# An attention kernel on one core: the probabilities' product with the mask is read from SBUF and stands behind the split of the next weights, and two late tiles' values are moved on

## The chip, the cores and the metric

The kernel runs on one core of one Trainium2 chip. The metric is device time in microseconds (us) of one execution of the whole program. A core has five engines with a queue each, which are worked in order: TensorE (PE in the profile; its weight loads are PEld), VectorE (DVE), ScalarE (ACT), GpSimd (POOL) and SyncE (SP). SP and POOL issue the DMA transfers here. The memory on the core is SBUF; TensorE's results land in PSUM.

## The reference

One step of a small decoder for a prompt of 1024 positions and 8 single-token samples, model width 2048, all in float32. With the sizes of this case it has one pooling layer and one attention layer. The attention layer is the one that the change touches:

```python
z = x @ w_in                                   # queries (32 heads x 64) and gate
q = rope_partial(z[..., :D_ATTN], pos)         # rotation of 16 of 64 dimensions
s = einsum('qkgd,skd->kgqs', q, k) * 64 ** -0.5
s = where((kp <= qp) & (qp - kp < 128), s, -1e30)        # window of 128
m = maximum(max(s), sink)
p = exp(s - m);  p = p / (sum(p) + exp(sink - m))
o = einsum('kgqs,skd->qkgd', p, v)
y = (o * silu(gate)) @ w_out
x = layer_norm(ALPHA * x + y)
```

Keys and values are shared by groups of 8 heads and are projected once.

## The kernel before, in words

**Tiling.** Activations lie transposed: channels on the 128 partitions, positions along the free dimension, in two chunks c = 0 (512 columns) and c = 1 (512 columns and the 8 samples). The program runs through ten phases. Each phase multiplies a stream of weight blocks (128 x 1024) with one chunk. A float32 product is made of three faster ones: every weight block is cast by ScalarE to a high part (line 488, `cast_to`), VectorE takes the rest (line 503, the "split", in `prep_to`), and TensorE multiplies high by high, high by low and low by high (lines 658 to 660, or 686 to 688).

**Runs and units.** Most phases use Strassen's scheme with seven products: one `run` is one weight block, 24 matmuls. Two phases are "plain": there a `unit` makes one output tile from two blocks of 24 matmuls. The attention projections are three phases: chunk 0, heads tiles t = 0 to 7 (plain), chunk 0, t = 8 to 15 (seven products), and chunk 1, t = 0 to 15 (seven products). A tile t is two heads.

**What sets the order.** The program is written out in full by Python, and each engine's order is the order in which the functions record. A step counter `self.i` goes on by one at `end()`: after each run, and twice within each block of a unit (so a unit is four steps). `begin()` starts a block: it flushes `posts` (evictions of the last results and the like), loads blocks ahead on SP's queue, casts and splits the next block (`prep_to`), and casts further ahead. `end()` puts in TensorE's side work that is due at this step (`product`, by rank) and then the other engines' (`at`).

**Attention beside the projections.** `attend(c, t, at, s1, s2, late)` puts a tile's attention between the projections' runs, at steps counted from its call: `score` (line 1760, TensorE, into the PSUM tile `S`) at step `at`; `select` and `largest` (lines 1778 to 1790), `expo`, `total`, `norm` (lines 1797 to 1810) in the next steps; `turn` (line 1814, eight transposes into `PT`, the first half of `S`) at `at + s1`; `keep`; and `values0` (line 1848) at `at + s1 + s2`. `keep` makes two SBUF tiles from `PT`: ScalarE's copy `w` (line 1823) and VectorE's product with a constant mask, `wp` (line 1824). With s2 = 2 `keep` is recorded at the end of the step after the transposes, with s2 = 1 it is put into `posts`. `values` has two parts; each needs `w` for its first four matmuls and `wp` from the fifth on. Part 1 comes after part 0, and in many steps the next tile's score stands between them. `late` says where the values land in PSUM: in the second half of `S`, or in tiles of their own. `gate` (line 1876) then multiplies with the gate.

**Rotation.** A query pair's halves are exchanged by DMA (line 1616, on SP's queue); VectorE then makes the rotation, two products (line 1624) and a sum (line 1731), and a small copy for the samples (line 1735). `q_done` records it three steps after the projection, at the end of a step. The next score needs it.

**Sums of weight blocks.** The seven products need sums of blocks. They are made by VectorE the first time (line 293 in the plain phase, line 346 in the next one, with a store on POOL's queue) and read back later; for the output projection they are made on the side (lines 436 to 441).

Of the kernel before, what the change touches and what calls it, by code (L numbers as in the profile page):

```python
# [16 lines left out]
P = 128  # L17
# [77 lines left out]
class Slot:  # L95


    def __init__(self, mem, i, h, a):
        self.mem, self.i, self.h, self.a = mem, i, h, a
# [82 lines left out]
class Kern:  # L182
    def __init__(self, ctx, tc, io):
        self.tc, self.io = tc, io
        self.nc = tc.nc
        pool = lambda name, **kw: ctx.enter_context(tc.tile_pool(name=name, **kw))
        one = pool("one", bufs=1)
        self.smp = pool("smp", bufs=2)
        dram = pool("dram", bufs=1, space=bass.MemoryType.DRAM)
        self.psd = [pool(f"psd{i}", bufs=1, space=bass.MemoryType.PSUM) for i in range(3)]  # L190
        self.pso = pool("pso", bufs=1, space=bass.MemoryType.PSUM)
        self.four = None
        ctx.callback(self.use_four, None)
        self.prm = one.tile([P, N_PRM], F32, name="prm")
        self.cst = one.tile([P, N_CST], F32, name="cst")
        self.mki = one.tile([P, P], I32, name="mki")
        self.jr = one.tile([P, P], F32R, name="jr")
        self.nsink = one.tile([P, NH], F32, name="nsink")
        self.carry = one.tile([P, NK, NST], F32, name="carry")
        self.kdec = one.tile([P, 2, NDEC], F32, name="kdec")  # L200
        self.qd = [one.tile([P, NDEC, 8], F32, name=f"qd{i}") for i in range(2)]
        self.sgd = [one.tile([P, 8, NDEC], F32, name=f"sgd{i}") for i in range(2)]
        self.flag = one.tile([P, 1], F32, name="flag")
        self.mem = Mem(pool("mem", bufs=1), NSLOT)
        self.n = 0
        self.i = self.e = self.lastO = self.turns = self.ring = 0
        self.posts, self.events, self.side = [], {}, []
        self.extra, self.on = None, False
        self.fresh = False
        self.ahead = 7, 4, 3  # L210
        dr = lambda n, s: dram.tile(s, F32, tag=n, name=n)
        self.Td, self.act, self.l_sq, self.l_sh = {}, {}, {}, {}
        for c, (_, T) in enumerate(CHUNKS):
            for n, k in (("x", "ai"), ("g", "ao"), ("h", "bi"), ("o", "bo")):
                if (k, c) in STRASSEN:
                    self.Td[n, c] = dr(f"t{n}{c}", [P, 8, 4, T // 2])
            self.act["x", c] = io[f"x{c}"]
            for n in ("g", "h", "o", "p"):
                self.act[n, c] = dr(f"{n}{c}", [P, NK, T])
        self.gbd = dram.tile([32, 2 * P], F32, tag="gbd", name="gbd")  # L220
        self.ws = {
            n: [dr(f"s{n}{q}", [P, 4, 1024]) for q in range(np_)]
            for n, np_ in (("wia", 16), ("woa", 8), ("wkv", 2), ("wib", 16), ("wob", 8))
        }
# [285 lines left out]
    def flush(self):  # L510
        todo, self.posts = self.posts, []
        for go in todo:
            go()

    def begin(self):
        self.flush()
        a, b, d = self.ahead if self.strassen else (5, 4, 3)
        if getattr(self, "ph", "") == "bi1" and len(self.mem.whole()) < 4:
            a, b, d = min(a, 6), min(b, 3), min(d, 2)
        self.load_to(self.e + a)  # L520
        self.prep_to(self.e + d)
        self.cast_to(self.e + b)
        self.make_to(self.e + b + (1 if self.strassen else 0))
        self.e += 1
        return self.hl.pop(self.e - 1)
# [146 lines left out]
    def unit(self, done):  # L672

        nc = self.nc
        ps = self.psD()
        for par in range(2):
            w = self.begin()
            wh, wl = (s.r for s in w)
            for k in range(8):
                if k == 4:  # L680
                    self.flush()
                s = slice(k * P, (k + 1) * P)
                if k % 2 == 0:
                    x = self.x_get((par, k // 2))
                h, l = (a.rv(2, TP)[:, k % 2, :] for a in x)
                nc.tensor.matmul(ps[:], wh[:, s], h, start=par == 0 and k == 0, stop=False)  # L686
                nc.tensor.matmul(ps[:], wh[:, s], l, start=False, stop=False)  # L687
                nc.tensor.matmul(ps[:], wl[:, s], h, start=False, stop=par == 1 and k == 7)  # L688
                if k % 2:
                    self.x_used((par, k // 2))  # L690
                if k == 7:
                    for a in w:
                        a.free()
                    if par == 1:
                        self.posts.append(lambda: done(ps))
                if k in (3, 7):
                    self.end()
# [1047 lines left out]
    def attend(self, c, t, at, s1, s2, late=False):  # L1745
# [5 lines left out]
        PT = self.S[:, 0, :]  # L1751
        x = {}
# [66 lines left out]
        def keep():  # L1819


            x["w"], x["wp"] = self.mem.full(), self.mem.full()
            nc.scalar.copy(x["w"].a[:, :1024], PT)
            nc.vector.tensor_mul(
                x["wp"].a[:, :1024].rearrange("p (i k) -> p i k", k=P),
                PT.rearrange("p (i k) -> p i k", k=P),
                cst[:, None, K_MP : K_MP + P].to_broadcast([P, 8, P]),
            )

# [30 lines left out]
                x["wp"].free()  # L1860

        def values0():
            values(0)
            if self.i in self.scores:
                self.product(0, 3, lambda: values(1))
                self.at(1, gate)
            else:
                self.product(1, 0, lambda: values(1))
                self.at(1, lambda: self.posts.append(gate))
# [27 lines left out]
        if s2 > 1:  # L1897
            self.at(at + s1 + 1, keep)
        else:
            self.at(at + s1, lambda: self.posts.append(keep))  # L1900
        self.product(at + s1 + s2, 1, values0)

    def gate_done(self, c, t0, s, n):
# [125 lines left out]
    def phase_bi(self, c, ps, nxt):  # L2029
# [4 lines left out]
        if not self.strassen:  # L2034
            for done in (self.k_done, self.v_done):
                box = {}
                for j in range(2):

                    def take(ps, j=j, done=done, box=box):
                        if j == 0:  # L2040
                            box["s"] = self.mem.full()
                        nc.scalar.copy(box["s"].a[:, j * T : (j + 1) * T], ps[:])
                        if j == 1:
                            done(c, box["s"])

                    self.unit(take)
            for t in range(2 * ps[0], 2 * ps[-1] + 2):
                def q_done(ps, t=t):
                    s = self.mem.half()
                    nc.scalar.copy(s.a[:, :T], ps[:])  # L2050
                    self.q_done(c, t, s, 1, 4)

                def g_done(ps, t=t):
                    s = self.mem.half()
                    nc.scalar.copy(s.a[:, :T], ps[:])
                    self.gate_done(c, t, s, 1)

                n = t - 2 * ps[-1]
                self.attend(c, t, 9, *{-1: (11, 1), 0: (13, 2), 1: (8, 2)}.get(n, (14, 2)), n == 0)
                self.unit(q_done)  # L2060
                if t == 2 * ps[-1] - 1:
                    self.x_begin(nxt)
                self.last = t == 2 * ps[-1] + 1
                self.unit(g_done)
            self.last = False
            return
# [295 lines left out]
```

## Time and profile before

| what | value |
|---|---|
| median of 3 runs | 2360.27 us (2354.43, 2361.5, 2360.27) |
| the profiled execution's own time | 2356.38 us |
| its span, first to last instruction | 2354.6 us |
| TensorE busy | 2297.3 us, 98% of the span |
| VectorE busy | 1925.9 us, 82% |
| ScalarE busy | 1343.1 us, 57% |
| mean granted TensorE clock | 0.996 |
| attention beside the projections | about 1158 to 2040 us |

In a row of a group, the numbers behind the bar are the busy time, the mean duration of one in ns, and the idle time of the engine just before them, with what ended most of it. In a row of waits, "A <- B: x, n, m" says that A waited x us for B in n waits, the longest m. In a timeline the columns are start in us, duration in us, engine, line, operation, tiles and shapes, count, and in square brackets the idle time before, with what ended it; rows of one kind are merged. A row of windows has the stretch, its length, the busy time and instructions of PE, PEld, DVE, ACT and POOL, the granted clock, the DMA engines' share and GB/s.

### The profile page before, as it was taken

The numbers are of one execution on the slowest core, as the hardware profiler recorded it, in microseconds if no ns is written. First come the engines' busy times: TensorE is split into PE (matmuls) and PEld (weight loads), VectorE is DVE, ScalarE is ACT, GpSimd is POOL, SyncE is SP. The second block draws the span as 40 slices with busy tenths as digits, with TensorE's granted clock in tenths as the row PEclk, the third lists the DMA queues.
The fourth block names the chain that finished last, engine by engine and source line by source line (L and its number), as shares of the span: only waits on it lengthen the run. The fifth ranks groups of instructions, "written<-read, shape, count | busy, mean of one in ns | idle before, by whom it ended". The sixth has DMA issues, their size and how long they took to land. (4 is left out here: it accounts for less than half of the span.)

```text
span 2354.6 us, 49710 instructions
## 1 busy us (share of the span) xinstructions
PE 2297.3 (98%) x19960; PEld 2200.9 (93%) x19960; DVE 1925.9 (82%) x2421; ACT 1343.1 (57%) x2429; POOL 205.5 (9%) x411
## 2 busy tenths in 40 slices
PE   8999999999999999999999899999999999999997
PEld 6899999999999999998788799999999999999997
DVE  8787998776878878978987788887777768888887
ACT  4444446544546547554465566685666678546556
POOL 0111110001000000000111111100000000000000
PEclk9999999999999999999999999999999999999999
DMA  8668789989889989999786766688777768799785
GB/s 293 211 246 303 271 299 346 332 292 319 289 289 339 327 280 333 328 388 327 272 310 220 248 219 239 224 310 270 237 249 245 230 201 305 239 342 372 260 300 199
DMA packets 250919, 665.18 MB, mean 283 GB/s; under 512 B 25632, under 2 KB 106432, under 8 KB 250688
## 3 DMA queue, kind: packets, MB, share of 16 engines
q1 hardware_dynamic: 205216, 496.94, 63.0%
q0 software_dynamic: 45472, 165.07, 18.1%
q8 instruction: 156, 2.56, 0.4%
q14 instruction: 75, 0.61, 0.1%
HBM read 466.81 MB, written 185.59 MB: 277 GB/s over the span
## 5 line engine op out<-in xcount | busy, mean ns | idle before, releaser
L658 PE MATMUL pD<-m,m 128*128 128x260 f32 (+1 forms) x4752 | 1346.0, 283 | 8.1 <-ACT pD L599 4.4
L660 PE MATMUL pD<-m,m 128*128 128x260 f32 (+1 forms) x4752 | 1339.1, 282 | 4.4 <-DVE m L503 4.4
L659 PE MATMUL pD<-m,m 128*128 128x260 f32 (+1 forms) x4752 | 1338.8, 282 | 0.0
L658 PEld LDWEIGHTS pD<-m,m 128*128 128x128 f32 x4752 | 894.5, 188 | 13.7 <-ACT pD L599 5.5
L660 PEld LDWEIGHTS pD<-m,m 128*128 128x128 f32 x4752 | 895.2, 188 | 5.5 <-DVE m L503 5.5
L503 DVE TENSOR_TENSOR m<-m,m 128x1024 fp32r<-128x1024 f32 x674 | 814.5, 1219 | 100.1 <-ACT m L488 60.6
L659 PEld LDWEIGHTS pD<-m,m 128*128 128x128 f32 x4752 | 894.9, 188 | 0.5
L488 ACT CAST m<-m 128x1024 fp32r<-128x1024 f32 x674 | 702.7, 1049 | 324.7 <-DVE m L346 85.1
L686 PE MATMUL pD<-m,m 128*128 128x512 f32 x448 | 179.7, 401 | 8.0 <-ACT m L769 8.0
L687 PE MATMUL pD<-m,m 128*128 128x512 f32 x448 | 177.9, 397 | 1.0 <-DVE m L778 1.0
L688 PE MATMUL pD<-m,m 128*128 128x512 f32 x448 | 177.5, 396 | 0.0
L778 DVE TENSOR_TENSOR m<-m,m 128x1024 fp32r<-128x1024 f32 (+1 forms) x120 | 147.0, 1226 | 6.4 <-ACT m L769 4.7
L769 ACT CAST m<-m 128x1024 fp32r<-128x1024 f32 (+1 forms) x120 | 125.9, 1053 | 17.7 <-PE pD L687 5.2
L631 ACT COPY m<-pD 128x260 f32<-128x260 f32 (+1 forms) x83 | 31.1, 375 | 179.2 <-PE pD L660 179.1
L346 DVE TENSOR_TENSOR m<-m,m 128x1024 f32<-128x1024 f32 x88 | 107.6, 1222 | 12.7 <-DMA m<-in_wib 6.3
L686 PEld LDWEIGHTS pD<-m,m 128*128 128x128 f32 x448 | 85.1, 190 | 28.1 <-ACT m L769 8.0
L687 PEld LDWEIGHTS pD<-m,m 128*128 128x128 f32 x448 | 85.0, 190 | 21.1 <-DVE m L778 2.1
L688 PEld LDWEIGHTS pD<-m,m 128*128 128x128 f32 x448 | 85.0, 190 | 19.7
L1797 ACT ACTIVATE m<-m,sm 128x128 f32<-128x128 f32 x256 | 99.4, 393 | 0.0
L619 DVE TENSOR_TENSOR m<-pD,m 128x260 f32<-128x260 f32 (+1 forms) x86 | 36.5, 424 | 74.4 <-PE pD L660 74.1
L1088 PE MATMUL pD<-m,m 128*128 128x260 f32 (+1 forms) x528 | 91.5, 323 | 0.0
L1088 PEld LDWEIGHTS pD<-m,m 128*128 128x128 f32 x528 | 79.5, 188 | 8.2
(249 smaller groups left out, 2180.9 us busy)
## 6 DMA issues: line engine op xcount, KB each, us to landing
m<-in_wia SPq DMA_DIRECT2D x124, 512.0 KB
m<-in_wib SPq DMA_DIRECT2D x120, 512.0 KB
swia<-m POOLq DMA_DIRECT2D x64, 512.0 KB, 4.8
m<-swia SPq DMA_DIRECT2D x64, 512.0 KB
m<-swoa SPq DMA_DIRECT2D x64, 512.0 KB
swib<-m POOLq DMA_DIRECT2D x64, 512.0 KB, 5.1
m<-swib SPq DMA_DIRECT2D x64, 512.0 KB
m<-swob SPq DMA_DIRECT2D x56, 512.0 KB
```

The costliest lines, as they stand in the source:

```text
L346: self.nc.vector.tensor_add(s[out].a[:, :1024], s[x].a[:, :1024], s[y].a[:, :1024])
L488: self.nc.scalar.copy(hi.r[:, :1024], self.stream[self.cast].src().a[:, :1024])
L503: self.nc.vector.tensor_sub(lo.r[:, :1024], s.src().a[:, :1024], hi.a[:, :1024])
L658: nc.tensor.matmul(ps[:, :TH], wh[:, s], h, start=new and k == 0, stop=False, skip_group_check=on)
L659: nc.tensor.matmul(ps[:, :TH], wh[:, s], l, start=False, stop=False, skip_group_check=on)
L660: nc.tensor.matmul(ps[:, :TH], wl[:, s], h, start=False, stop=k == 7, skip_group_check=on)
L686: nc.tensor.matmul(ps[:], wh[:, s], h, start=par == 0 and k == 0, stop=False)
L687: nc.tensor.matmul(ps[:], wh[:, s], l, start=False, stop=False)
L688: nc.tensor.matmul(ps[:], wl[:, s], h, start=False, stop=par == 1 and k == 7)
L769: self.nc.scalar.copy(h.r[:, :n], s.a[:, :n])
L778: self.nc.vector.tensor_sub(l.r[:, :n], s.a[:, :n], h.a[:, :n])
L1088: nc.tensor.matmul(ps[:, : cs.stop - cs.start], ws[:, s], d[:, cs], start=f0 and k == 0, stop=l0 and k == 3,)
```

## The change

The mask product reads ScalarE's SBUF copy `w` instead of `PT`. It is no longer recorded in `keep`: `keep` puts it on a list, `behind_prep`, which a new function `settle` empties. `settle` is called in `begin()` behind `prep_to`, in `unit` behind the flush in the middle of a block, and ahead of the values. For the plain phase's tiles 5 (n = -1) and 6 (n = 0) the steps are changed: tile 5's transposes come two steps later, and its values land in the second half of `S`; tile 6's values follow one step behind the transposes instead of two.

```diff
@@ class Kern
+        self.behind_prep = []
...
+    def settle(self):
+        todo, self.behind_prep = self.behind_prep, []
+        for go in todo:
+            go()
+
     def begin(self):
         self.flush()
...
         self.load_to(self.e + a)
         self.prep_to(self.e + d)
+        self.settle()
         self.cast_to(self.e + b)
@@ def unit
                 if k == 4:
                     self.flush()
+                    self.settle()
@@ def keep
             nc.scalar.copy(x["w"].a[:, :1024], PT)
+            self.behind_prep.append(mask)
+
+        def mask():
             nc.vector.tensor_mul(
                 x["wp"].a[:, :1024].rearrange("p (i k) -> p i k", k=P),
-                PT.rearrange("p (i k) -> p i k", k=P),
+                x["w"].a[:, :1024].rearrange("p (i k) -> p i k", k=P),
                 cst[:, None, K_MP : K_MP + P].to_broadcast([P, 8, P]),
             )
@@ def values0
+            self.settle()
             values(0)
@@ def phase_bi
-                self.attend(c, t, 9, *{-1: (11, 1), 0: (13, 2), 1: (8, 2)}.get(n, (14, 2)), n == 0)
+                self.attend(c, t, 9, *{-1: (13, 1), 0: (13, 1), 1: (8, 2)}.get(n, (14, 2)), n in (-1, 0))
```

How this moves instructions is seen in the engines' orders. The changed file is longer, so its line numbers are higher: the mask is line 1824 before and 1835 in the changed kernel, ScalarE's copy 1823 and 1831, the cast 488 and 489, the split 503 and 504, the rotation 1624 and 1632 with its sum 1731 and 1739 and its copy 1735 and 1743, a sum of weight blocks 346 and 347, an eviction 619 and 626. A row is line, operation, result <- operands (the numbers tell buffers apart) and shape.

VectorE in chunk 1, at the transposes of tile 2 (the place is the mask of `keep` and what follows), before:

```order
L503 TENSOR_TENSOR m_2213_20135<-m_2197_19966,m_2210_20090 128x1024
L1824 TENSOR_TENSOR m_2216_20164<-pS_12840,cst 128x1024
L1624 TENSOR_TENSOR m_2188_19835<-m_2188_19835,m_1533_12852 128x1040
L1624 TENSOR_TENSOR m_2203_20041<-m_2203_20041,m_1533_12852 128x1040
L1731 TENSOR_TENSOR m_2188_19835<-m_2188_19835,m_2203_20041 128x1040
L1735 COPY qd_82<-m_2188_19835 128x8x2
L619 TENSOR_TENSOR m_2217_20175<-pD_20046,m_2207_20084 128x260
```

and of the change:

```order
L504 TENSOR_TENSOR m_2213_20133<-m_2197_19964,m_2210_20088 128x1024
L1632 TENSOR_TENSOR m_2188_19832<-m_2188_19832,m_1533_12852 128x1040
L1632 TENSOR_TENSOR m_2203_20039<-m_2203_20039,m_1533_12852 128x1040
L1739 TENSOR_TENSOR m_2188_19832<-m_2188_19832,m_2203_20039 128x1040
L1743 COPY qd_82<-m_2188_19832 128x8x2
L1835 TENSOR_TENSOR m_2216_20162<-m_2215_20161,cst 128x1024
L626 TENSOR_TENSOR m_2217_20172<-pD_20044,m_2207_20082 128x260
```

The mask has moved behind the whole rotation of the next queries, since `keep` and the rotation are recorded at the end of the same step and `settle` only in the next `begin()`.

VectorE in chunk 0, at the transposes of tile 8, before:

```order
L503 TENSOR_TENSOR m_1847_16223<-m_1827_15972,m_1846_16186 128x1024
L1824 TENSOR_TENSOR m_1850_16252<-pS_12840,cst 128x1024
L1624 TENSOR_TENSOR m_1826_15970<-m_1826_15970,m_1533_12852 128x1024
L1624 TENSOR_TENSOR m_1838_16134<-m_1838_16134,m_1533_12852 128x1024
L1731 TENSOR_TENSOR m_1826_15970<-m_1826_15970,m_1838_16134 128x1024
L503 TENSOR_TENSOR m_1853_16266<-m_1835_16098,m_1848_16225 128x1024
```

and of the change:

```order
L504 TENSOR_TENSOR m_1847_16221<-m_1827_15970,m_1846_16184 128x1024
L1632 TENSOR_TENSOR m_1826_15968<-m_1826_15968,m_1533_12852 128x1024
L1632 TENSOR_TENSOR m_1838_16132<-m_1838_16132,m_1533_12852 128x1024
L1739 TENSOR_TENSOR m_1826_15968<-m_1826_15968,m_1838_16132 128x1024
L504 TENSOR_TENSOR m_1853_16263<-m_1835_16096,m_1848_16223 128x1024
L1835 TENSOR_TENSOR m_1850_16250<-m_1849_16249,cst 128x1024
```

Here the mask stands behind the rotation and behind the split of the next block.

ScalarE around the copy of tile 5 in the plain phase, before:

```order
L488 CAST m_1736_15001<-m_1731_14947 128x1024
L1795 ACTIVATE sm_14990<-sm_14990 128x8
L1797 ACTIVATE m_1734_14967,sm_14991<-m_1734_14967,sm_14989 128x128 x4
L769 CAST m_1739_15037<-m_1697_14586 128x1024
L1823 COPY m_1742_15043<-pS_12840 128x1024
L1797 ACTIVATE m_1734_14967,sm_14991<-m_1734_14967,sm_14989 128x128 x4
L769 CAST m_1745_15086<-m_1729_14943 128x1024
L488 CAST m_1750_15100<-m_1722_14842 128x1024
```

and of the change:

```order
L489 CAST m_1736_15001<-m_1731_14947 128x1024
L1803 ACTIVATE sm_14990<-sm_14990 128x8
L1805 ACTIVATE m_1734_14967,sm_14991<-m_1734_14967,sm_14989 128x128 x4
L777 CAST m_1739_15029<-m_1697_14586 128x1024
L1805 ACTIVATE m_1734_14967,sm_14991<-m_1734_14967,sm_14989 128x128 x4
L777 CAST m_1743_15055<-m_1729_14943 128x1024
L489 CAST m_1748_15069<-m_1722_14842 128x1024
L1831 COPY m_1750_15095<-pS_12840 128x1024
```

The copy has moved behind four exponentials and two casts. The last of these casts reads a block (m_1722_14842) that VectorE makes by a sum, line 346 before and 347 now.

VectorE at the same place, of the change, from the sum that reads the block loaded last:

```order
L347 TENSOR_TENSOR m_1731_14947<-m_1730_14945,m_1731_14947 128x1024
L294 TENSOR_TENSOR m_1685_14484<-m_1685_14484,m_1718_14790 128x1024
L786 TENSOR_TENSOR m_1738_15027<-m_1692_14538,m_1728_14941 128x1024
L294 TENSOR_TENSOR m_1693_14540<-m_1685_14484,m_1693_14540 128x1024
L786 TENSOR_TENSOR m_1742_15053<-m_1697_14586,m_1739_15029 128x1024
L504 TENSOR_TENSOR m_1747_15063<-m_1731_14947,m_1736_15001 128x1024
L347 TENSOR_TENSOR m_1730_14945<-m_1722_14842,m_1730_14945 128x1024
L347 TENSOR_TENSOR m_1722_14842<-m_1722_14842,m_1731_14947 128x1024
```

Before, the mask stood behind the third of these rows (the one with m_1738); now it is not among these eight, and comes four rows later.

## The prediction

> **What bounds the kernel now.** I read the page first, then TensorE's waits in the attention stretch, then the groups of the two lines that the change touches.
>
> ```profile
> span 2354.6 us, 49710 instructions
> PE 2297.3 (98%) x19960; PEld 2200.9 (93%) x19960; DVE 1925.9 (82%) x2421; ACT 1343.1 (57%) x2429; POOL 205.5 (9%) x411
> ...
> PE pS L1760 <- DVE m L1731: 8.4, 8, 1.5
> PE pO L1848 <- ACT m L1823: 7.8, 1, 7.8
> ...
> PE pS L1848 <- DVE m L1824: 1.5, 3, 0.7
> ...
> PE pO L1848 <- DVE m L1824: 0.6, 1, 0.6
> ...
> L1824 DVE TENSOR_TENSOR m<-pS,cst x32: 1216/1225/1227, 1203.7 to 2030.4; 128x1024 f32<-128x1024 f32 x32
> ...
>   ACT m L1823: 46.5, 25
>   PE pD L659: 9.0, 4
> ```
>
> TensorE is busy for 2297.3 of 2354.6 us, so time is won or lost only where TensorE stands still. The four wait rows are the ones on which this change can act, 18.3 us in all between 1130 and 2040 us, 0.8% of the span: scores that wait for the rotated queries (L1731), values that wait for ScalarE's copy (L1823) or for the mask (L1824). The last rows are the mask's own group: 32 masks of 1.225 us, and VectorE stood idle 46.5 us in front of 25 of them because ScalarE's copy of the same PSUM tile had to end first. That idleness costs nothing by itself; it costs where a split or a rotation behind the mask is late for TensorE.
>
> I number a turn n = 16c + t (chunk c, tile t).
>
> **The mask's read.** It now reads the SBUF copy. The copy must therefore still end first, so the 46.5 us of order "copy, then mask" stay; only what VectorE does meanwhile changes. The duration I take as unchanged: a split, SBUF to SBUF in the same shape, takes
>
> ```profile
> L503 DVE TENSOR_TENSOR m<-m,m 128x1024 fp32r<-128x1024 f32 x674 | 814.5, 1219 | 100.1 <-ACT m L488 60.6 <-issue 13.2 <-PE pD L659 8.6
> ```
>
> 1.219 against 1.225 us: 32 x 0.006 us is nothing.
>
> **The mask's place, turns with a rotation whose rows come late.** The order shows that the mask is moved past more than the split: in the even turns the rotation of the next two query tiles (L1624 twice, L1731) now stands ahead of it, and often the split too. TensorE's order there is values part 0 (which needs the mask after its first four matmuls), then the next score (which needs L1731). Turn 18 before:
>
> ```profile
> 1711.27 2.49 SPq L1616 DMA_DIRECT2D m<-m  x4
> ...
> 1717.96 1.23 DVE L1824 TENSOR_TENSOR m<-pS,cst 128x1024 f32<-128x1024 f32 x1 [1.11 <-ACT m L1823]
> 1720.21 2.39 DVE L1624 TENSOR_TENSOR m<-m,m 128x1040 f32<-128x1040 f32 x2 [1.02 <-DMA m<-m]
> 1722.63 1.24 DVE L1731 TENSOR_TENSOR m<-m,m 128x1040 f32<-128x1040 f32 x1
> ...
> 1723.99 0.42 DVE L619 TENSOR_TENSOR m<-pD,m 128x260 f32<-128x260 f32 x1
> ...
> 1722.46 0.22 PE L1848 MATMUL pO<-m,m 64*64 64x64 f32 x2
> ...
> 1723.93 0.39 PE L1760 MATMUL pS<-m,m 64*64 64x192 f32 x4 [0.84 <-DVE m L1731]
> ```
>
> The mask ran inside the wait for the partner rows' DMA, which ended at 1720.21. Now it stands behind the rotation and its small copy (L1735), where L619 stood: 1723.99 to 1725.22. The matmuls that read it (1722.46 before) wait until 1725.25. From the first of them to the score it takes 0.45 us without a wait, as in turn 0:
>
> ```profile
> 1207.15 0.22 PE L1848 MATMUL pO<-m,m 64*64 64x64 f32 x2
> ...
> 1207.60 1.48 PE L1760 MATMUL pS<-m,m 64*64 64x192 f32 x32
> ```
>
> So the score starts at 1725.70 instead of 1723.93: 1.77 us lost; the wait for L1731 (0.84) is replaced by a longer one for the mask. The same in turns 20, 24 and 12, whose rotations also waited for the DMA:
>
> ```profile
> 1771.01 2.40 DVE L1624 TENSOR_TENSOR m<-m,m 128x1040 f32<-128x1040 f32 x2 [1.65 <-DMA m<-m]
> ...
> 1871.68 2.39 DVE L1624 TENSOR_TENSOR m<-m,m 128x1040 f32<-128x1040 f32 x2 [0.24 <-DMA m<-m]
> ...
> 1527.05 2.36 DVE L1624 TENSOR_TENSOR m<-m,m 128x1024 f32<-128x1024 f32 x2 [0.88 <-DMA m<-m]
> ...
> 1530.59 1.22 DVE L503 TENSOR_TENSOR m<-m,m 128x1024 fp32r<-128x1024 f32 x1
> 1531.72 1.24 DVE L778 TENSOR_TENSOR m<-m,m 128x1040 fp32r<-128x1040 f32 x1
> ...
> 1531.35 0.33 PE L1760 MATMUL pS<-m,m 64*64 64x192 f32 x1
> ```
>
> Turns 20 and 24 again 1.77 each. In turn 12 the split comes too, the mask starts where L778 stood, 1531.72, ends at 1532.94, and the score starts at 1533.42 instead of 1531.35: 2.07. Sum 7.4 us lost.
>
> **Turns 8, 10, 16, 22, 26, 28.** Here the rotation had been held by the mask alone. Turn 8:
>
> ```profile
> 1417.17 2.42 SPq L1616 DMA_DIRECT2D m<-m  x4
> ...
> 1428.88 1.23 DVE L1824 TENSOR_TENSOR m<-pS,cst 128x1024 f32<-128x1024 f32 x1 [2.48 <-PE pD L659]
> 1430.02 2.35 DVE L1624 TENSOR_TENSOR m<-m,m 128x1024 f32<-128x1024 f32 x2
> ...
> 1433.55 1.22 DVE L503 TENSOR_TENSOR m<-m,m 128x1024 fp32r<-128x1024 f32 x1
> ...
> 1433.68 0.56 PE L1760 MATMUL pS<-m,m 64*64 64x192 f32 x8 [1.14 <-DVE m L1731]
> ```
>
> The rotation can start 2.48 + 1.14 us earlier (1.14 is the mask's share of the queue, 1428.88 to 1430.02), if its rows have landed: from issue to landing they took 8.9 us in turn 18 (1711.27 to 1720.21), so issued at 1417.17 they are there at about 1426.1, in time for 1426.40. Then comes the split, and the mask starts at 1433.55 - 2.48 = 1431.07, ends at 1432.30, the score at 1432.78: 0.9 won, and 0.8 in turn 10, which looks the same. If the rows came only at 1430.02, the mask would start at 1434.69 and 2.7 would be lost. By the same two ends the others are
>
> ```profile
> 1669.08 1.23 DVE L1824 TENSOR_TENSOR m<-pS,cst 128x1024 f32<-128x1024 f32 x1 [1.28 <-ACT m L1823]
> ...
> 1674.80 1.22 DVE L503 TENSOR_TENSOR m<-m,m 128x1024 fp32r<-128x1024 f32 x1
> ...
> 1820.74 1.23 DVE L1824 TENSOR_TENSOR m<-pS,cst 128x1024 f32<-128x1024 f32 x1 [0.91 <-ACT m L1823]
> ...
> 1966.52 1.23 DVE L1824 TENSOR_TENSOR m<-pS,cst 128x1024 f32<-128x1024 f32 x1 [1.24 <-ACT m L1823]
> ```
>
> turn 16: +1.3 (late rows +3.7); 22: -0.3 to +1.8, I take 1.1; 26: 0 to +2.8, 0.3; 28: +0.4 to +2.8, 0.4. Turn 7 has no idle time to fill, so rotation and split together put its mask 2 x 1.14 us back and its score some 1.6 behind; the gate of tile 6, now a run earlier, gives VectorE about 1 us of that back: +0.6. With -1.7 for turns 8 and 10 the sum is +2.0 us, ends -0.5 and +16.
>
> **Odd turns, and tiles whose values follow after one run.** Odd turns have no rotation and 1.8 to 3.3 us between the mask's end and its reader, so a split ahead costs nothing. In turns 6, 13, 14, 29, 30 and 31 the values come one run behind the transpose. Their wait for the mask's PSUM read (the 1.5 us row) ends, but the mask stands one split later (at most 1.14 us). Ends: -1.5 and 6 x 1.14 - 1.5 = +5.3; since the split mostly fills the time of the copy, I take +1.
>
> **Turn 5, the tile moved on.** Its 7.8 us wait is TensorE's longest:
>
> ```profile
> 1328.94 1.22 DVE L346 TENSOR_TENSOR m<-m,m 128x1024 f32<-128x1024 f32 x1 [5.75 <-DMA m<-in_wib]
> ...
> 1332.80 1.03 ACT L769 CAST m<-m 128x1024 fp32r<-128x1024 f32 x1
> 1333.73 1.00 ACT L1823 COPY m<-pS 128x1024 f32<-128x1024 f32 x1
> ...
> 1323.17 1.03 PE L1814 MATMUL pS<-cst,m 128*128 128x128 f32 x8
> 1334.79 0.48 PE L1848 MATMUL pO<-m,m 64*64 64x128 f32 x2 [7.79 <-ACT m L1823]
> ...
> 1327.00:1346.00 19.00, 10.66 (x94) 8.36 (x95) 14.62 (x19) 10.56 (x28) 3.59 (x8) 0.73 0.95 295
> ```
>
> A weight block landed at 1328.94; ScalarE's queue stood behind its sum, and the copy with it. Now TensorE goes on with two more half weights (2.8 us each) and reaches the values at about 1332.5 instead of 1327.0. But on ScalarE the copy now stands behind one more cast, of a block that VectorE finishes eighth from the landing: the rows at 1328.94 and after run 1.14 us apart and one waits for the cast of 1332.80, so that sum ends at about 1338.5, the cast runs 0.94, the copy 1339.5 to 1340.5, the mask to 1341.8. TensorE again waits some 8 us, only later in its own work. The stall also halves the clock: 0.73 over 19 us is 10.3 us at half speed, 5.8 of them in work (1334.8 to 1340.6), 2.9 us lost. I take -1 for the whole turn; ends -11.2 (7.8 + 0.6 + 2.9, all gone) and +2.
>
> [...]
>
> **Sum.** 7.4 + 2.0 + 1 - 1 = 9.4 us lost. The moved copies, sums and DMA issues are as many as before; what runs earlier on VectorE is covered by TensorE's own work. The profiled execution took 2356.4 us, 3.9 under the median of the three runs (2360.3); the mean of the four is 2358.1, on which 9.4 gives 2368.
>
> **Rivals.** [...]
> *The rotated rows arrive early: faster.* One mechanism: if they land within 4 us of the last issue, the rotation fills the wait for the copy in turns 18, 20, 22 and 24 too, the mask is done before its reader, and the score waits go: about -5 in place of +7.4, total -4 with turn 5 as above and down to -10 with some gain there: 2350. It decides at landing by 1716.9 in turn 18; the row says 1720.2.
> *Rows later still: slower by more.* Late ends in turns 8, 10, 16, 26, 28 (+14 in place of about 0): 2379. [...]
> *The change does not do what it says:* the mask behind the rotation, not just the split, is in my forecast already and has no chance of its own.
>
> **Chances.** Forecast 0.52, no change 0.20, faster 0.14, slower by more 0.14. About 0.3%, 7 us, can be told from no change. A quarter of the forecast's spread (4 to 15 us) lies under it: slower 0.39 + 0.14 = 0.53; same 0.13 + 0.20, less 0.02 by which the no-change case may pass 7 us of gain, 0.31; faster 0.16. The range, 2352 to 2379, takes in part of both outer cases; the forecast's own is 2362 to 2373.
>
> **What would show it.** Right: the wait row of L1760 on L1731 nearly gone, a new row of L1848 on L1835 (the mask) of 12 us or more with single waits of 2 to 3 us in turns 12, 18, 20, 24, and turn 5's wait still about 8 us. Wrong: waits on the mask under 4 us in all, or turn 5's wait under 4.

## The result and the profile after

| | before | changed |
|---|---|---|
| median, six runs each (us) | 2357.94 | 2371.23 |
| lowest to highest | 2354.43 to 2361.5 | 2365.7 to 2374.59 |
| ratio of the times | | 1.0052 (95% interval 1.0039 to 1.0064) |
| profiled execution, time and span | 2356.38, 2354.6 | 2368.8, 2367.0 |

The change makes the kernel 0.5% slower, about 12 us. The span of the profiled execution grew by 12.4 us. First the head of the page of the changed kernel, then TensorE's waits from 1130 to 2060 us (us in sum, how many, the longest):

```profile
span 2367.0 us, 49710 instructions
PE 2301.5 (97%) x19960; PEld 2203.7 (93%) x19960; DVE 1927.7 (81%) x2421; ACT 1341.8 (57%) x2429; POOL 205.1 (9%) x411
```

```profile
PE pO L1859 <- DVE m L1835: 11.9, 8, 3.2
PE pS L1859 <- ACT m L1831: 7.0, 1, 7.0
PE pS L1859 <- DVE m L1835: 2.8, 4, 1.5
PE pS L1768 <- DVE m L1739: 2.7, 3, 1.5
PE pD L665 <- DVE m L626: 1.8, 1, 1.8
PE pD L1859 <- POOL flag L1867: 1.7, 4, 1.2
```

The score's wait for the rotation fell from 8.4 to 2.7 us. The values' wait for the mask, in two rows, rose from 1.5 + 0.6 to 2.8 + 11.9 us. Turn 5's wait for ScalarE's copy is still there, 7.0 for 7.8 us. TensorE stands idle 47.8 us over the whole span, summed over the gaps between its matmuls, where it stood idle 40.0 before. That is 7.8 of the 12.4 us.

Most of the rest is clock. The windows view (length, busy time of each engine, then the granted clock, the DMA share and GB/s) around turns 5, 12 and 22, of before and then of the changed kernel:

```profile
1310.00:1340.00 30.00, 21.65 (x199) 17.00 (x198) 21.39 (x24) 10.42 (x25) 4.22 (x10) 0.84 0.85 263
1524.00:1546.00 22.00, 20.35 (x239) 19.71 (x239) 18.35 (x21) 17.60 (x34) 0.96 (x3) 1.00 1.04 365
1820.00:1840.00 20.00, 19.37 (x255) 18.80 (x255) 16.72 (x22) 12.26 (x28) 0.66 (x2) 1.00 0.63 189
```

```profile
1320.00:1350.00 30.00, 22.42 (x167) 18.74 (x166) 21.32 (x26) 15.80 (x38) 4.20 (x10) 0.89 0.96 311
1530.00:1552.00 22.00, 17.93 (x197) 16.41 (x196) 18.14 (x21) 14.94 (x28) 0.95 (x3) 0.84 1.05 381
1825.00:1845.00 20.00, 16.76 (x219) 15.74 (x218) 12.29 (x19) 8.00 (x16) 0.66 (x2) 0.91 0.53 162
```

Where the clock is not 1.00 in these stretches it is 0.50, so half speed lasts 2 x (1 - clock) x length. In the profile before it came, while the attention ran, only in turn 5, for 10.2 us (0.50 from 1330.36 to 1340.60 us). Now it is 6.8 us in turn 5, 6.8 us in turn 12 (0.84 over 22 us) and 3.4 us in turn 22 (0.91 over 20 us). A score's matmul took 0.089 us at half speed in turn 12 (24 in 2.14 us) and 0.046 us at full speed in turn 24 (32 in 1.48 us). TensorE worked for 12.5 us of these stretches where it had worked for 5.3 us of the one before; by an estimate from these numbers half of the difference, 3.6 us, is lost. Turn 22 in the changed kernel, VectorE and then the matmul that reads the mask:

```profile
1828.40 2.40 DVE L1632 TENSOR_TENSOR m<-m,m 128x1040 f32<-128x1040 f32 x2 [2.93 <-DMA m<-m]
1830.84 1.24 DVE L1739 TENSOR_TENSOR m<-m,m 128x1040 f32<-128x1040 f32 x1
1832.11 0.17 DVE L1743 COPY qd<-m 128x16 f32<-128x16 f32 x1
1832.19 1.22 DVE L1835 TENSOR_TENSOR m<-m,cst 128x1024 f32<-128x1024 f32 x1
...
1833.47 0.27 PE L1859 MATMUL pO<-m,m 64*64 64x64 f32 x2 [3.24 <-DVE m L1835]
```

VectorE stands idle 2.93 us for the rotation's partner rows, with the mask queued behind the whole rotation. TensorE waits 3.24 us for the mask. Turn 12 has the split in the queue too, and two waits with 0.44 us of matmuls between them:

```profile
1532.54 0.44 PE L1859 MATMUL pD<-m,m 64*64 64x128 f32 x4 [1.57 <-ACT m L621]
1535.13 0.37 PE L1859 MATMUL pO<-m,m 64*64 64x64 f32 x2 [2.15 <-DVE m L1835]
```

VectorE's own waits between 1130 and 2060 us show the same exchange. The first row is before, the two others the changed kernel:

```profile
DVE m L1624 <- DMA m<-m: 7.7, 5, 3.9
```

```profile
DVE m L1632 <- DMA m<-m: 21.5, 8, 4.7
DVE m L1835 <- ACT m L1831: 15.7, 12, 3.8
```

The mask's wait for the copy fell from 46.5 to 15.7 us, as something now fills it. The rotation's wait for its rows rose from 7.7 to 21.5 us, since the mask used to fill that one.

### The profile page after: what moved, and what is told of

It is laid out like the page before. It is cut to its first block, busy times and chain, and to the rows that moved or that the text cites. A ratio compares the mean times of both kernels' runs of the same rounds, so it can differ in the third digit from the quotient of the medians.

```text
span 2367.0 us, 49710 instructions
## 1 busy us (share of the span) xinstructions
PE 2301.5 (97%) x19960; PEld 2203.7 (93%) x19960; DVE 1927.7 (81%) x2421; ACT 1341.8 (57%) x2429; POOL 205.1 (9%) x411
## 5 line engine op out<-in xcount | busy, mean ns | idle before, releaser
L666 PE MATMUL pD<-m,m 128*128 128x260 f32 (+1 forms) x4752 | 1339.5, 282 | 0.0
```

Of the source, the lines that this page charges most:

```text
L666: nc.tensor.matmul(ps[:, :TH], wh[:, s], l, start=False, stop=False, skip_group_check=on)
```

## The experiments

The theory: the mask stands behind the rotation, so where the partner rows land late the values wait for rows that they do not need, and the longer waits also halve the clock. The rivals: the moved tiles 5 and 6 cost the time; the split ahead of the mask does; the read from SBUF does.

### The parts of the change apart

`e1_mask_only` keeps the tiles' steps as before; `e2_tiles_only` changes only them; `e3_sbuf_read` changes only the operand.

```diff
 e1, in the changed kernel:
-*{-1: (13, 1), 0: (13, 1), 1: (8, 2)}.get(n, (14, 2)), n in (-1, 0))
+*{-1: (11, 1), 0: (13, 2), 1: (8, 2)}.get(n, (14, 2)), n == 0)
 e2, in the kernel before: the same two lines, exchanged
 e3, in the kernel before:
-                PT.rearrange("p (i k) -> p i k", k=P),
+                x["w"].a[:, :1024].rearrange("p (i k) -> p i k", k=P),
```

> The changed kernel with the plain tiles' steps as they were (only the mask's read and place are changed). Theory 1 (the mask standing behind the rotation makes the values wait, and two of these waits throttle the clock): about as slow as the full change, 10 to 14 us over the kernel before; values waiting for the mask 12 us or more in sum; the clock at half in turns 12 and 22. Rival (the moved tiles 5 and 6 cost the time): within 3 us of before.

> The kernel before with only the two plain tiles' steps changed. Theory 1: within 3 us of before, since the turn-5 stall only moves (one wait of 6 to 8 us there). Rival (the moved tiles cost the time): 6 us or more over before.

> The kernel before with the mask's product reading the SBUF copy, in its old place. Prediction: no difference (within 2 us of before), the mask 1.21 to 1.23 us and still behind the copy. Rival (two readers of PSUM cost time, or the read from SBUF does): 5 us or more either way.

| | median (us) | before on the same chip | ratio, 95% interval |
|---|---|---|---|
| e1, mask only | 2371.12 | 2357.34 | 1.0058 (1.0045 to 1.0072) |
| e2, tiles only | 2360.92 | 2357.34 | 1.0015 (1.0006 to 1.0023) |
| e3, SBUF read only | 2357.78 | 2358.31 | 0.9996 (0.9985 to 1.0008) |

The mask alone costs all of it. TensorE's waits in e1:

```profile
PE pO L1859 <- DVE m L1835: 16.4, 11, 4.4
PE pO L1859 <- ACT m L1831: 6.8, 1, 6.8
```

Moving the two tiles costs about 3.5 us, more than the 3 us bound that e2 was given. In its profile the turn-5 wait is 8.1 us (now put down to the mask behind the copy) and turn 5 is followed by another 3.4 us at half speed, from 1367.9 us. The two parts do not add up to the whole (13.7 + 3.5 against 12), but the intervals leave room for that. The read from SBUF costs nothing: in e3 the mask took

```profile
L1824 DVE TENSOR_TENSOR m<-m,cst x32: 1221/1226/1228, 1204.7 to 2031.5; 128x1024 f32<-128x1024 f32 x32
```

1.226 us, and VectorE still waited 45.7 us for the copy in front of it.

### The mask's place

```diff
 e4, in the changed kernel, at the start of the rotation:
         def b():
+            self.settle()
             t = box["t"]
 e6, in the changed kernel, in begin():
         self.flush()
+        self.settle()
...
         self.prep_to(self.e + d)
-        self.settle()
```

> The changed kernel, with the mask put back ahead of the rotation in the turns that have one; in the other turns it still stands behind the split, and it reads SBUF everywhere. Theory 1: 0 to 3 us over before, waits of values on the mask 3 us or less in sum, half clock in turn 5 alone. Rival (the split ahead of the mask in the turns without rotation): 6 us or more over before. Rival (the read from SBUF, or another order of transfers): about as slow as the full change, 12 us.

> The changed kernel, with the mask ahead of the split but still behind the rotation. If rotation and split each cost their 1.1 to 3.6 us of queue: turns 20, 22 and 24 keep their waits (7 us), turns 8, 10, 12, 16 and 28 lose one split's 1.1 us or what they wait, turn 12 is no longer throttled: 5 to 9 us over before. If the rotation alone costs it: 10 to 13 us over. If the split alone costs it: within 2 us of before.

e4 took 2359.47 us, ratio 1.0006 (0.9996 to 1.0015): the loss is gone. e6 took 2367.34 us, 1.0038 (1.0023 to 1.0053): 9 to 10 us over before, at the border of the first two outcomes that were set down for it. TensorE's waits, e4 and then e6:

```profile
PE pS L1769 <- DVE m L1740: 7.3, 6, 2.3
PE pS L1860 <- ACT m L1832: 7.3, 1, 7.3
PE pS L1860 <- DVE m L1836: 2.2, 3, 1.5
```

```profile
PE pO L1859 <- DVE m L1835: 8.2, 4, 3.2
PE pS L1859 <- ACT m L1831: 6.9, 1, 6.9
```

In e4 the row of values in `pO` waiting for the mask is gone and the score's wait is back at 7.3 us. So the rotation ahead of the mask is the cause. One part of the expectation missed: half clock came not in turn 5 alone, but also behind it (3.4 us from 1368.3 us) and in turn 22 (3.4 us from 1829.1 us), there behind the score's wait of 2.3 us. The split ahead of it adds 3 to 4 us: in e6 four waits of 1.0 to 3.2 us remain in the `pO` row, in turns 12, 20, 22 and 24 (8.2 us), where eight made 11.9. Turn 12 was expected at full clock there; its profile has 3.4 us at half speed, from 1536.0 us. e6 and the full change differ by 0.0014 with intervals that overlap, so that the size of the split's share rests on the profile.

### The clock

`e7_filler` puts work into the two waits behind which the clock was halved:

```diff
+            if part == 0 and (c, t) in ((0, 12), (1, 6)):
+                for _ in range(12):
+                    nc.tensor.matmul(
+                        x["o"][0][:, :P], x["w"].a[:, :P], x["w"].a[:, P : 2 * P], start=True, stop=False,
+                        skip_group_check=True,
+                    )
```

> The changed kernel, with twelve more TensorE products (128x128, into a part of the result that the first values' matmul overwrites) ahead of the values' matmuls of turns 12 and 22, so that TensorE works while it waits for the mask; some 2.9 us each if one takes the 0.24 us of a values' matmul. If the waits there also cost a halved clock, and TensorE's standing still is what halves it: no half clock near 1533 and 1834 us, 2.6 + 1.7 = 4.3 us less than the full change, so about 8 us over before. If the halved clock has another cause or small products don't hold it: as slow as the full change, 12 to 13 us over, or more by what the filler overruns the wait.

2366.48 us, 1.0032 (1.0018 to 1.0045): 8.2 over before, 4.7 less than the full change by the ratios. By the times alone that difference is not certain (the intervals overlap), but the windows view of the two stretches shows where it comes from:

```profile
1530.00:1552.00 22.00, 19.73 (x238) 19.02 (x236) 18.69 (x21) 14.69 (x28) 0.96 (x3) 1.00 1.05 370
1825.00:1845.00 20.00, 20.00 (x262) 19.36 (x261) 14.48 (x20) 10.23 (x18) 0.66 (x2) 1.00 0.61 186
```

The clock is 1.00 in both. Measured by how much later than before the next turn's transposes come, turn 12 now costs 3.1 us in place of 5.1, and turn 22 2.0 in place of 4.3: together 4.3 less, in sum what the two halved stretches were priced at (2.6 + 1.7). The clock of all timed executions agrees: its mean is 0.9932 in the six of the changed kernel, 0.9953 in the nine of e7, and 0.995 in the kernel before. The 0.0021 between the first two stand for 2 x 0.0021 x 2367 = 9.9 us at half speed, and the two stretches were 6.8 + 3.4 us. So in these two turns the clock was halved where TensorE stood still (0.84 and 0.91) and not where the filler kept it at work (1.00 and 1.00), and by the trace, matmuls that compute nothing wanted make the two turns 4.3 us shorter.

### The partner rows

If late rows are the cause, earlier rows must heal the change. `e9_rows_other_queue` issues them on POOL's queue; `e10_rows_before` does the same to the kernel before.

```diff
-            self.nc.sync.dma_start(t.a[32 * a : 32 * a + 32, : n * T], s.a[32 * b : 32 * b + 32, : n * T])
+            self.nc.gpsimd.dma_start(t.a[32 * a : 32 * a + 32, : n * T], s.a[32 * b : 32 * b + 32, : n * T])
```

> The changed kernel, with the rotation's partner rows issued on POOL's queue in place of SP's. If the mask is late because these rows land late (turns 12, 20, 22, 24) and the rows now land before the transposes end: the rotations start 0.3 us behind the transposes in all turns, the values wait 5 us or less for the mask in sum, no half clock in turns 12 and 22, 7 to 12 us less than the full change. If they land as late on this queue: as slow as the full change. If POOL's queue then holds up its flag or the stores: new waits there, and slower.

> The same edit on the kernel before. There the rotation stands behind the mask, so rows that land early win only the score's waits of turns 12, 18, 20 and 24 (the rotation's 0.2 to 1.7 us): 0 to 4 us faster than before. If the queue is as late or holds up others: no difference or slower.

e9: 2363.1 us, 1.0015 (1.0004 to 1.0027), 8 to 9 us less than the full change with no change in VectorE's order. VectorE's wait for the rows and TensorE's for the mask:

```profile
DVE m L1632 <- DMA m<-m: 8.1, 6, 2.4
```

```profile
PE pO L1859 <- DVE m L1835: 5.7, 5, 2.6
PE pS L1859 <- DVE m L1835: 2.7, 4, 1.5
```

The rows' wait is back from 21.5 to 8.1 us. In turns 12, 20 and 24 the rotation starts at the latest 0.3 us behind the transposes' end, and the mask is in time; turns 12 and 22 keep the full clock. In turn 22 the rows are still late (2.3 us) and the mask with them (2.6 us). The waits sum to 8.4 us, where 5 was expected. In turn 16, where the rows now keep VectorE waiting 0.8 us, the values wait 1.95 us, and 3.4 us at half speed follow. e10: 2359.16 us, 1.0001 (0.999 to 1.0011), no difference. There the rotations of turns 12, 18, 20 and 24 no longer wait for their rows, but the score's waits still sum to 8.8 us, 4.9 of them in turn 22.

### Tile 5

Both edits are in the kernel before. `e5_tile5_earlier` puts tile 5's transposes one run earlier; they then land in PSUM before tile 6's scores are read there, so tile 6's probabilities are not the reference's, while the instructions are the same. `e8_tile5_values_later` leaves transposes and copy, and puts the values one half block later.

```diff
-*{-1: (11, 1), 0: (13, 2), 1: (8, 2)}.get(n, (14, 2)), n == 0)
 e5:
+*{-1: (10, 1), 0: (13, 2), 1: (8, 2)}.get(n, (14, 2)), n == 0)
 e8:
+*{-1: (11, 2), 0: (13, 2), 1: (8, 2)}.get(n, (14, 2)), n == 0)
```

> The kernel before with tile 5 moved the other way: its transposes one run earlier, so that ScalarE's copy stands ahead of the cast that waits for the block landed last. If the turn-5 stall comes from the copy's place behind late casts (the prediction's step): the wait of 7.8 us goes, the half clock with it, 7 to 11 us faster than before. If another late weight takes its place within the next blocks, the wait moves there: 0 to 4 us faster. If the transposes wait for the reading of the next tile's scores: about 2 us of the gain are lost.

> The kernel before with tile 5's transposes and copy where they were and its values one half block (2.8 us) later. If the copy's end (1334.7 us) is what TensorE waits for: the wait falls from 7.8 to about 5 us, 2.8 to 4.5 us faster. If moving the values moves the wait along, as in the change: no difference from before.

e5 took 2359.9 us, 1.0001 (0.9988 to 1.0014), and e8 2357.74 us, 0.9996 (0.9985 to 1.0008): neither makes a difference that can be told, so both expected gains (7 to 11 and 2.8 to 4.5 us) did not come. In e5 the copy ran ahead of the late cast, and TensorE's next long wait came later, for another copy of ScalarE's queue:

```profile
1324.62 1.01 ACT L1823 COPY m<-pS 128x1024 f32<-128x1024 f32 x1 [1.73 <-DVE m L1782]
1329.68 1.05 ACT L488 CAST m<-m 128x1024 fp32r<-128x1024 f32 x1 [4.04 <-DVE m L346]
...
1344.02 0.58 PE L658 MATMUL pD<-m,m 128*128 128x256 f32 x1 [3.53 <-ACT m L2055]
```

In e8 the wait was 3.88 us (about 5 expected), but a new one of 1.0 us for the gate came behind it, and the profile of e8 has turn 12's wait for ScalarE and a halved clock there. The late block holds ScalarE's whole queue, so that moving one reader moves the wait. By the turns' ends e8 won 1.6 us and e5 4.3 us around turn 5 and gave them back in later turns of their profiled executions; whether by the shift or by chance is open. Even the gain is not shown to be the edits': e3, e10 and e11 leave tile 5 as it was, and against the same profile of before they are 1.6, 0.9 and 4.6 us shorter there. In e11 no row of VectorE waits for the late block, and TensorE waits 1.7 us for the copy.

### Placed by turn

`e11_by_turn` uses the mask's place behind the rotation only in turns whose rows had landed early in the profiles (turn 28 but for 0.75 us at most):

```diff
 in e6, with the tiles' steps as before, in keep() and at the start of the rotation:
             self.behind_prep.append(mask)
+            self.turn = 16 * c + t
...
+            if self.behind_prep and self.turn not in (8, 10, 16, 28):
+                self.settle()
             self.rope(s, t, n, T)
```

> The mask reads SBUF and stands behind the rotation, ahead of the split, in turns 8, 10, 16 and 28 alone, where the rows had landed early in every run so far; in all others it stands ahead of rotation and split, and tiles 5 and 6 keep their steps. Prediction: 1.7 + 0.6 + 0.8 us won in turns 8, 10 and 16, about 3 us faster than before. If these gains come from the moved tiles instead: no difference.

2355.36 us (12 runs), ratio 0.9988 (0.9977 to 0.9999): about 2.7 us faster than before, just told apart from none. In turn 8 rotation, mask and split now follow each other without a gap:

```profile
1426.64 2.35 DVE L1632 TENSOR_TENSOR m<-m,m 128x1024 f32<-128x1024 f32 x2
1429.02 1.23 DVE L1741 TENSOR_TENSOR m<-m,m 128x1024 f32<-128x1024 f32 x1
1430.17 1.22 DVE L1838 TENSOR_TENSOR m<-m,cst 128x1024 f32<-128x1024 f32 x1
1431.30 1.22 DVE L504 TENSOR_TENSOR m<-m,m 128x1024 fp32r<-128x1024 f32 x1
```

Its median is the lowest of the kernels here. Its profiled execution was the slowest of its twelve (2363.43 us), so that its trace tells the order and not the whole gain. The three turns themselves won 0.6, 0.4 and 0.5 us in it against the profile before, 1.4 us in sum where 3.1 were expected; where the rest of the 2.7 us comes from is open.

## Why the prediction was right, by its steps

It forecast 2368 us, slower by 9.4; measured were 2371, slower by 12 to 13. The direction and the mechanism are as it put them, and so are the waits' rows, near enough: the rotation's row fell to 2.7 of 8.4 us ("nearly gone"), the mask's two rows make 14.7 us (12 or more), turn 5's wait is still 7 us. Of the single waits of 2 to 3 us, those of turns 12 and 24 came; turn 20 waited 1.8 us, turn 18 not, and turn 22 the longest. e4, e6 and e9 show the cause. Its terms, against how much each turn of the profiled execution shifted (the start of the next turn's transposes, after less before):

| term of the sum | forecast | measured |
|---|---|---|
| turns 12, 18, 20, 24 | +2.07, 3 x 1.77 = 7.4 | +5.1, -1.1, +0.4, +2.3 = 6.7 |
| turns 7, 8, 10, 16, 22, 26, 28 | +2.0 | -1.56, -0.57, -0.35, +0.30, +4.27, -0.06, +0.94 = +3.0 |
| turns 6, 13, 14, 29, 30, 31 | +1 | +0.9, of it +1.6 in turn 6 |
| turn 5 | -1 | +0.2 |
| other odd turns | 0 | -0.6 |
| ahead of turn 5 | 0 | +2.1 |
| sum | 9.4 | 12.3 of the span's 12.4 |

The table sets one execution against one. Five profiles have the mask in its old place and the rows on SP's queue (before, e2, e3, e5, e8). Against the profile of before, turn 22 is 0 to 4.5 us longer in them, turn 12 between 0.2 us shorter and 2.6 longer, turn 18 up to 1.1 and turn 20 up to 1.6 shorter; e3 and e5 have 3.4 us at half speed in turn 22, e5 and e8 in turn 12. So that profile was a good one in turns 12 and 22 and a bad one in turns 18 and 20. Against the mean of the five, the changed kernel and e1 lost 3.5 us in turn 12, 3.3 in turn 22, 2.2 in turn 24, 1.2 in turn 0, 1.0 in turn 20 and 0.3 in turn 18.

**Turns 12 and 22** are the mis-sized terms: 5.1 for 2.07 and 4.3 for 1.1 (3.5 and 3.3 against the mean). Of turn 12 the half clock is 2.6 us, of turn 22 1.7, half of TensorE's work in the stretches (5.26 and 3.41 us); with the clock kept, in e7, the two turns are 2.0 and 2.2 us shorter. The step that failed: the forecast's terms price a halved clock in turn 5 alone. No run shows that every wait of 2 to 3 us keeps the full clock; in the changed kernel the clock was 0.50 from 1533.56 us on, within the second of turn 12's waits (1.57 and 2.15 us), and from 1833.94 us on, behind turn 22's of 3.24 us.

**Turn 18** was to lose 1.77 and won 1.1. Of the four turns whose rows were late before, the rival "the rotated rows arrive early" held there, and only there:

```profile
1722.82 2.38 DVE L1632 TENSOR_TENSOR m<-m,m 128x1040 f32<-128x1040 f32 x2
1725.24 1.24 DVE L1739 TENSOR_TENSOR m<-m,m 128x1040 f32<-128x1040 f32 x1
1726.51 0.18 DVE L1743 COPY qd<-m 128x16 f32<-128x16 f32 x1
1726.60 1.22 DVE L1835 TENSOR_TENSOR m<-m,cst 128x1024 f32<-128x1024 f32 x1
```

The rotation starts without a wait. In e1 the rows of the same turn kept VectorE waiting 2.43 us: one execution's landing was read as the turn's own. In turns 20, 22 and 24 the rows were late in the profiles of the change, e1 and e6.

**Turns 8, 10 and 28** went the forecast way; their rows were there when the rotation could start, but for 0.4 us in turn 28. Turn 16 lost 0.3 us and not 1.3. Turn 6 lost 1.6 us and turn 7 won 1.6, since tile 6's values and gate moved across the line between them: e1, without that move, has 0.0 and +0.7 (0.6 forecast for turn 7), e2, with it alone, +1.1 and -1.2.

**Turn 5.** The copy was forecast at 1339.5 to 1340.5 and the mask to 1341.8, with TensorE waiting some 8 us. VectorE, ScalarE and TensorE there:

```profile
1336.90 2.48 DVE L347 TENSOR_TENSOR m<-m,m 128x1024 f32<-128x1024 f32 x2
...
1339.47 1.04 ACT L489 CAST m<-m 128x1024 fp32r<-128x1024 f32 x1 [2.39 <-DVE sm L1812]
...
1340.42 1.00 ACT L1831 COPY m<-pS 128x1024 f32<-128x1024 f32 x1
...
1341.48 0.71 PE L1859 MATMUL pS<-m,m 64*64 64x128 f32 x8 [7.03 <-ACT m L1831]
```

The chain is the one forecast, a microsecond later in a program that ran 2.1 us later by then. The cast's sums end at 1339.38; the profile names a small instruction (L1812) that ended just behind them. The gain of 1 us did not come: over turn 5 the kernel lost 0.2 us here, and 3.2 in e2. A large gain in turn 5, the case of no change among the chances, needed the late block sooner; its sum started at 1329.70, 0.8 us later than before, and e5 and e8 found no place near it that is better by what the runs can tell.

**Not priced** were the 2.1 us ahead of turn 5. About 1.1 are a gap at 1007 us, ahead of the attention, that other kernels show in other sizes; 1.2 are turn 0, where the second part of the values now waits 1.16 us for POOL's flag (L1867), in all profiles in which the mask stands behind the rotation of that turn.

So the sum was nearer than its terms, and that is luck: the half clock made up for turns 18 and 20, which cost less. Two sums of the prediction do not come out of its own terms: the ends of the turns from 7 to 28 make +0.3 and about +17 (not -0.5 and +16), and the late rows make about 2381 us (not 2379). The second is the upper end of the range, which the measured time does not come near.

## What to carry to other kernels

An instruction whose operands are there early is good cover in front of one that waits for a transfer; moved behind it, it inherits the transfer's lateness and hands it on to its own readers (here the values' waits for the mask rose from 2.1 to 14.7 us). Before moving work past a waiting instruction, read for each place whether that wait ends early or late, in more than one execution, and move it only where it ends early (e11). Price a new wait of TensorE with the clock that it may lose behind it: here 3.4 us at half speed followed a wait of 1.8 us behind turn 5 in e2 and e4, and none the one of 1.75 us there in the changed kernel (clock 1.00 from 1366 to 1378 us).

## What was unexpected of the hardware

The clock was halved by waits far shorter than turn 5's of 7.0 us, and not by every one of them. In the changed kernel the stretches at half speed begin at 1339.00, 1533.56 and 1833.94 us and last 6.8, 6.8 and 3.4 us. In turn 20 of e6 a wait of 2.11 us halved the clock; in turn 20 of e7 one of 2.48 us did not. For each of the two waits, the matmul that waited and the windows view of the 20 us around it (the clock is the number ahead of the last two), e6 first:

```profile
1778.26 0.33 PE L1859 MATMUL pO<-m,m 64*64 64x64 f32 x2 [2.11 <-DVE m L1835]
```

```profile
1770.00:1790.00 20.00, 17.89 (x207) 16.97 (x206) 12.87 (x16) 9.60 (x17) 0.65 (x2) 0.91 0.73 234
```

```profile
1780.22 0.27 PE L1865 MATMUL pO<-m,m 64*64 64x64 f32 x2 [2.48 <-DVE m L1835]
```

```profile
1770.00:1790.00 20.00, 17.52 (x218) 17.00 (x217) 13.49 (x15) 10.10 (x18) 0.66 (x2) 1.00 0.82 269
```

In the same way 2.33 us in turn 22 of e4 halved the clock (0.89 from 1825 to 1840 us), and 2.34 us in turn 24 of the changed kernel did not (1.00 from 1880 to 1905 us). So the length of a wait alone does not tell whether it costs the clock; what else decides is not shown here.

The landing of the partner rows differs between executions of nearly the same program by 2 us and more (in turn 18 VectorE waited 2.43 us for them in e1 and not at all in the changed kernel), which is more than most terms of the sum.
